# One block of a hybrid encoder in 3-pass fp32: first and last gate/up pair by products in turn, down's space in four pools, loads of the second half ahead of the last sums

## The chip, the cores and the metric

The kernel runs on one core of a Trainium2 chip. The metric is the time of one execution in device microseconds, the median of several runs. TensorE (PE) multiplies, VectorE (DVE), ScalarE (ACT) and GpSimd (POOL) do elementwise work, SyncE (SP) issues the DMAs of this part of the kernel. Each engine has a queue of its own and takes it in order.

## The reference

One layer with SEQ 2048, D 1024 and FF 2816 in float32; the kernel's third phase, which the change touches, ends it:

```python
x = x + merged @ w_out
h2 = rmsnorm(x, norm2_g)
x = x + (jax.nn.silu(h2 @ w_ffn_gate) * (h2 @ w_ffn_up)) @ w_ffn_down
return rmsnorm(x, norm_f_g)
```

Ahead of it stand an input projection, windowed attention and a bidirectional state-space scan, whose gated sum is `merged`.

## The kernel before

Products of fp32 matrices are made in three passes of fp32r (high by high, high by low, low by high). `hi_lo` (L828, L829) makes the two parts: ACT writes the rounded high part, DVE subtracts it for the low part. Names like H, w and zs are such pairs; `raw` is what a DMA brought. gate, up and down are computed with seven block products instead of eight, named BLK = ("11","S2","S1","12","S3","S4","22"); the operands S1 to S4 and the weights' block sums T (POOL, L847 to L850) are sums of quarters.

**Half by half.** The 2048 tokens are two halves of 1024. For each half `h_blocks` loads the seven H blocks from DRAM as 14 loads `hr` of 512 KB, each into one of three raw buffers that the weights' loads share, and splits them (14 roundings H on ACT, 14 on DVE). `gate_up` then goes through 22 units, that is 11 pairs of a gate unit and an up unit. A unit is seven products of 12 matmuls of 128x512. In `gu_unit` the products of "11" and "12" go to the PSUM tile ps_pj, "S2", "S3", "22" to ps_b, "S1" and "S4" to ps_a; between them c1 (L889, ACT), u2 (L892), c5 (L895), u3 (L900), u2 (L902) and, last, c1 (L907) take the partial sums out. Gate's results go through Silu on ACT (L944), up's are multiplied by them (L948). `z_blocks` makes from a pair the seven blocks of the next operand: three directly, four with sums on POOL (zsum, L926 to L931); each is split (zs) and stored to DRAM as z. `w_unit` loads, sums and splits the weights of a unit one unit ahead.

**Start of half 0.** The last quarter's x is normed by `norm_hs(3)`: four scalings of 128x1024 (L449 on ACT, L451 on DVE in the first phase), transposes on PE (L796), evictions hf (L797) and stores h. The first four H blocks are in before; S4 and 22 of them need h of this last quarter.

**Half 1's operand.** The sums S1 to S4 of half 1 are made by `h_sums_later` in four parts, after units 3, 6, 9 and 12 of half 0. After all of half 0 `h_blocks` asks for the H of half 1.

**Down.** `down` goes through 6 chunks of 8 units; a unit loads one z (three buffers, two units ahead) and makes seven products, in the first chunk of 3 matmuls each (4.8 us of TensorE a unit), later of 6. It keeps 16 tiles x and 8 tiles c1 over all chunks; the first chunk fills them (L1005, L1007, L1014).

**Space.** The pool gh holds the first four H blocks (8 x 8 KB a partition), gi the last three (6 x 8 KB), gt the tiles t (14 x 2 KB) and zs (3 x 4 KB). When they are closed, one pool "dn" takes their space for z, w3, x, c1, ct and gf. A tile of a new pool waits for every reader and writer of the space under that pool.

**Order.** The program is a list of instructions in the order of the code; a scheduler of the framework sets each engine's queue from it, by when operands come free. So the order on an engine isn't the code's word for word, but it is fixed when the kernel is built.

## Time and profile before

| | |
|---|---|
| median of 3 runs | 2749.73 us (2746.26 to 2751.05) |
| profiled execution | 2742.25 us, its span 2740.4 us |
| mean granted TensorE clock | 0.977 |
| PE busy | 2569.3 us, 94% |
| DVE, POOL, ACT busy | 1898.2, 1271.0, 1031.9 us |

The profile comes from one execution; its times within the span are used for differences, and a difference is set against the median. Gate/up of half 0 runs from about 1380 to 1860 us of the span, half 1 from there to 2281 us, down from there to the end. A wait is the idle time of an engine ahead of an instruction, with what ended it.

### The profile page before, as it was taken

The page shows a single profiled execution, that of the slowest core. Times are in us where ns is not written, and L with a number is a line of the kernel's source. Part 1 is how long each engine was busy: PE and PEld are TensorE (multiplying, and loading weights), DVE is VectorE, ACT ScalarE, POOL GpSimd, SP SyncE. Part 2 cuts the span into 40 slices and gives each one's busy share as a digit, 9 for nine tenths or more (in the row PEclk, how much of TensorE's full clock was granted, in tenths as well). Part 3 has the DMA queues.
Part 4 walks back from the last instruction along what each step waited for, and adds up shares of the span by engine and source line. Part 5 has one row for each costly group of instructions (what it writes and reads, how often), then busy time and mean ns, then how long its engine had stood idle before and what let it go on. Part 6 is the DMA issues. An engine that isn't in the chain of part 4 may idle for free.

```text
span 2740.4 us, 34681 instructions
## 1 busy us (share of the span) xinstructions
PE 2569.3 (94%) x12090; PEld 2115.4 (77%) x12090; DVE 1898.2 (69%) x2726; ACT 1031.9 (38%) x1877; POOL 1271.0 (46%) x1016
## 2 busy tenths in 40 slices
...
GB/s 161 98 143 183 183 128 74 94 78 105 77 176 180 184 170 146 165 203 238 188 211 169 177 180 172 155 180 199 154 152 150 162 155 200 254 270 253 217 190 257
DMA packets 451918, 467.95 MB, mean 171 GB/s; under 512 B 82848, under 2 KB 381856, under 8 KB 446624
## 3 DMA queue, kind: packets, MB, share of 16 engines
...
## 4 chain that ended last, share of the span: by engine, by line
PE 37%; DVE 5%; DMA 5%; POOL 4%; issue 3%; ACT 1%; SPq 0%; POOLq 0%; DVEq 0%; ACTq 0%
PE ps_b L876 15%; PE ps_a L876 10%; PE ps_pj L876 10%; DVE w L829 2%; DMA z<-z 1%; PE ps_pj L411 1%; DMA hr<-h 1%; PE ps_b L776 1%; PE ps_a L776 1%; POOL T L847 1%; DVE zs L829 1%; POOL T L848 1%; DMA raw<-in_w_ffn_up 1%; POOL T L849 1%; DVE H L829 1%
## 5 line engine op out<-in xcount | busy, mean ns | idle before, releaser
L411 PE MATMUL ps_pj<-h,w 128*128 128x512 f32 x1920 | 485.0, 401 | 0.0
L411 PEld LDWEIGHTS ps_pj<-h,w 128*128 128x128 f32 x1920 | 356.8, 189 | 79.1 <-issue 2.6
L876 PE MATMUL ps_b<-H,w 128*128 128x512 f32 x1584 | 386.4, 391 | 10.2 <-DVE u L892 5.2
L876 PEld LDWEIGHTS ps_b<-H,w 128*128 128x128 f32 x1584 | 297.7, 189 | 76.4 <-DVE u L900 7.9
L876 PE MATMUL ps_pj<-H,w 128*128 128x512 f32 x1056 | 265.0, 395 | 18.5 <-ACT c L889 17.7
L829 DVE TENSOR_TENSOR w<-T,w 128x512 fp32r<-128x512 f32 x220 | 205.1, 936 | 95.8 <-ACT w L828 93.5
L876 PE MATMUL ps_a<-H,w 128*128 128x512 f32 x1056 | 258.1, 390 | 1.0 <-ACT c L895 0.8
L876 PEld LDWEIGHTS ps_pj<-H,w 128*128 128x128 f32 x1056 | 200.4, 190 | 63.2 <-ACT c L889 20.1
L876 PEld LDWEIGHTS ps_a<-H,w 128*128 128x128 f32 x1056 | 198.2, 188 | 43.3 <-ACT c L895 2.2
L380 DVE TENSOR_TENSOR w<-raw,w 128x1024 fp32r<-128x1024 f32 x111 | 152.0, 1369 | 106.1 <-ACT w L377 77.2
L828 ACT ACTIVATE w<-T 128x512 fp32r<-128x512 f32 x220 | 136.0, 626 | 236.6 <-PE ps_b L876 74.7
L829 DVE TENSOR_TENSOR w<-raw,w 128x512 fp32r<-128x512 f32 x165 | 192.0, 1165 | 39.5 <-ACT w L828 39.5
L876 PE MATMUL ps_b<-w,z 128*128 128x512 f32 x792 | 202.8, 391 | 4.0 <-DVE xa L1009 3.1
L579 POOL TENSOR_SCALAR P<-P,st 128x384 f32<-128x384 f32 (+1 forms) x128 | 74.0, 597 | 270.6 <-DVE st L577 127.7
L876 PEld LDWEIGHTS ps_b<-w,z 128*128 128x128 f32 x792 | 148.6, 188 | 37.1 <-DVE xa L1009 4.5
L847 POOL TENSOR_TENSOR T<-raw 128x512 f32<-128x512 f32 x55 | 83.4, 1517 | 179.8 <-DVE w L829 117.4
L876 PE MATMUL ps_pj<-w,z 128*128 128x512 f32 x528 | 138.3, 393 | 19.8 <-DMA z<-z 19.2
L420 PE MATMUL ps_pj<-w,h 128*128 128x256 f32 x1152 | 147.7, 283 | 1.3 <-DVE h L463 0.8
L1009 DVE TENSOR_TENSOR xa<-xa,ps_b 128x512 f32<-128x512 f32 x128 | 87.1, 685 | 87.1 <-PE ps_b L876 85.4
L420 PEld LDWEIGHTS ps_pj<-w,h 128*128 128x128 f32 x1152 | 140.2, 188 | 3.5 <-issue 1.1
L571 DVE CUSTOM_DVE_ANT_0 P<-ps_a,cst,nsink 128x384 f32<-128x384 f32 (+1 forms) x128 | 74.1, 596 | 97.8 <-PE ps_a L569 97.4
L377 ACT ACTIVATE w<-raw 128x1024 fp32r<-128x1024 f32 x84 | 88.6, 1056 | 140.7 <-PE ps_pj L411 68.0
...
## 6 DMA issues: line engine op xcount, KB each, us to landing
...
```

The costliest lines, as they stand in the source:

```text
L377: self.s.activation(hi, src, AF.Copy)
L380: (lo_eng or self.v).tensor_tensor(lo, src, hi.bitcast(F32), SUB)
L411: self.pe.matmul(ps, W[a][:, k, cs], H[k][:, b, sl], start=(i == 0), stop=(i == n - 1))
L420: self.pe.matmul(ps, H[k][:, a, off:off + 128], W[k // 4][b][:, k % 4, :], start=(i == 0), stop=(i == n - 1))
L571: v.tensor_tensor_reduce(pt, sc, mk, -1.0, self.nsink[:, h:h + 1], ADD, ALU.min, nm[:, i:i + 1])
L579: p.tensor_scalar(P[i], P[i], den[:, i:i + 1], 1.0, MULT, MULT)
L776: self.pe.matmul(ps[t], M[k0 + k][:, a, 128 * t:128 * t + 128], W[b][:, k], start=(k0 + k + i == 0), stop=(k0 + k == 7 and i == 2))
L828: self.s.activation(hi, src, AF.Copy)
L829: self.v.tensor_tensor(lo, src, hi.bitcast(F32), SUB)
L847: eng.tensor_tensor(T[:, 0], b12, b11, SUB)
L876: self.pe.matmul(ps, a, b, start=(first and i == 0), stop=(i == n - 1), skip_group_check=True)
L1009: v.tensor_tensor(x[n], x[n], ps, ADD)
```

## The change

`gu_unit` becomes a generator that stops after each product. In the first and the last pair of each half (u = 0 and 20) gate's and up's products are taken in turn; for that up's weights and the next gate's are asked for ahead of the pair. The other pairs stay as they were. `gate_up` gets a function `after`, called after the last pair's products and ahead of its `z_blocks`: in half 0 it is `h_blocks` of half 1. `h_sums_later` comes after u = 2, 6, 10, 14, that is behind the pairs of units (2, 3), (6, 7), (10, 11) and (14, 15). In `norm_hs(3)` the four scalings of x and every second eviction hf go to DVE. Down's space is four pools: dz (three z) and dw (five w3) lie over gh, dm (x of the second half, ct, gf) over the end of gh and over gt, dx (x of the first half, c1) over gi. gf has three buffers.

```diff
--- before.py
+++ after.py
@@ -1,5 +1,6 @@
 import math
 from contextlib import ExitStack
+from itertools import zip_longest
 
 import numpy as np
 
@@ -58,6 +59,11 @@
     cst = np.concatenate([np.eye(128), mask, ka, km], 1)
     return (np.ascontiguousarray(rope.reshape(128, -1), dtype=np.float32),
             np.ascontiguousarray(cst, dtype=np.float32))
+
+
+def rest(gen):
+    for _ in gen:
+        pass
 
 
 class Kern:
@@ -435,7 +441,7 @@
         self.v.tensor_scalar(m, self.sumsq(x), 1.0 / D, 1e-6, MULT, ADD)
         return self.rsqrt(m)
 
-    def norm_x(self, src, tok, xs=None):
+    def norm_x(self, src, tok, xs=None, on_v=False):
 
         if xs is None:
             xs = []
@@ -445,7 +451,7 @@
                 xs.append(x)
         for x in xs:
             r = self.rstd(x)
-            if self.hi_on_act:
+            if self.hi_on_act and not on_v:
                 self.s.activation(x, x, AF.Copy, scale=r)
             else:
                 self.v.tensor_scalar(x, x, r, None, MULT)
@@ -786,7 +792,7 @@
     def norm_hs(self, q, X, g):
 
         hh, odd = divmod(q, 2)
-        self.norm_x(None, 0, X)
+        self.norm_x(None, 0, X, q == 3)
         for k in range(4):
             t = self.act.tile([128, 2, 512], F32, tag="a", name="hf")
             for i in range(2):
@@ -794,7 +800,10 @@
                 for j in range(4):
                     c = 128 * (k + 4 * i)
                     self.pe.transpose(pt[:, 128 * j:128 * j + 128], X[j][:, c:c + 128], self.ident)
-                self.s.activation(t[:, i], pt, AF.Identity, scale=g[:, k + 4 * i:k + 4 * i + 1])
+                if q == 3 and i:
+                    self.v.tensor_scalar(t[:, i], pt, g[:, k + 4 * i:k + 4 * i + 1], None, MULT)
+                else:
+                    self.s.activation(t[:, i], pt, AF.Identity, scale=g[:, k + 4 * i:k + 4 * i + 1])
                 if q != 1 or i:
                     self.store(self.hD[hh][f"{odd + 1}{i + 1}"][:, k], t[:, i])
             if q == 0:
@@ -887,20 +896,26 @@
         prod(A, "11", True, False)
         c1 = tl("c1")
         s.activation(c1, A, AF.Copy)
+        yield
         prod(B, "S2", True, False)
         u2 = tl("u2")
         v.tensor_tensor(u2, B, c1, ADD)
+        yield
         prod(C, "S1", True, False)
         c5 = tl("c5")
         s.activation(c5, C, AF.Copy)
+        yield
         prod(A, "12", False, True)
         fin("11", A)
+        yield
         prod(B, "S3", False, False)
         u3 = tl("u3")
         v.tensor_tensor(u3, B, c1, ADD)
+        yield
         prod(C, "S4", False, True)
         v.tensor_tensor(u2, C, u2, ADD)
         fin("12", u2)
+        yield
         prod(B, "22", False, True)
         p.tensor_tensor(u3, u3, c5, ADD)
         fin("22", u3)
@@ -932,26 +947,38 @@
         put("S3", Z["21"])
         put("S4", Z["12"])
 
-    def gate_up(self, tp, units, W, hh, H, nxt, bg):
+    def gate_up(self, tp, units, W, hh, H, nxt, bg, after=None):
+
 
         s, v, p = self.s, self.v, self.p
-        Z = {}
-        for u, (w, j) in enumerate(units):
-            Wn = self.w_unit(*units[u + 1]) if u + 1 < len(units) else nxt()
-            if u % 2 == 0:
-                def fin(n, z):
-                    g = tp.tile([128, 512], F32, tag="t", name="sg", bufs=14) if n == "11" else z
-                    s.activation(g, z, AF.Silu)
-                    Z[n] = g
+        n = len(units)
+        load = lambda u: self.w_unit(*units[u]) if u < n else nxt()
+        for u in range(0, n, 2):
+            Z = {}
+
+            def gate(n, z, Z=Z):
+                g = tp.tile([128, 512], F32, tag="t", name="sg", bufs=14) if n == "11" else z
+                s.activation(g, z, AF.Silu)
+                Z[n] = g
+
+            def up(n, z, Z=Z):
+                (p if n == "22" else v).tensor_tensor(Z[n], Z[n], z, MULT)
+
+            Wu = load(u + 1)
+            if u in (0, n - 2):
+                Wn = load(u + 2)
+                for _ in zip_longest(self.gu_unit(tp, W, H, gate), self.gu_unit(tp, Wu, H, up)):
+                    pass
             else:
-                def fin(n, z):
-                    (p if n == "22" else v).tensor_tensor(Z[n], Z[n], z, MULT)
-            self.gu_unit(tp, W, H, fin)
-            if u % 2:
-                self.z_blocks(tp, hh, j // 2, Z)
+                rest(self.gu_unit(tp, W, H, gate))
+                Wn = load(u + 2)
+                rest(self.gu_unit(tp, Wu, H, up))
+            if u == n - 2 and after:
+                H = after()
+            self.z_blocks(tp, hh, u // 2, Z)
             bg(u)
             W = Wn
-        return W
+        return W, H
 
     def wd_chunk(self, wd, j0, kc):
 
@@ -966,33 +993,33 @@
                 if self.nw % 16 < 11:
                     t = self.w_tile(self.nw % 16 if self.nw % 16 < 9 else 0, [128, 2, 512])
                 else:
-                    t = self.dp.tile([128, 2, 512], F32R, tag="w3", name="w", bufs=5)
+                    t = self.dw.tile([128, 2, 512], F32R, tag="w3", name="w", bufs=5)
                 self.nw += 1
                 self.hi_lo(t[:, 0], t[:, 1], src[n])
                 D7[n].append(t)
         return D7
 
-    def z_unit(self, dp, hh, c, tp, kc):
-
-        t = dp.tile([128, 7, 2, kc, 128], F32R, tag="z", name="z", bufs=3)
+    def z_unit(self, hh, c, tp, kc):
+
+        t = self.dz.tile([128, 7, 2, kc, 128], F32R, tag="z", name="z", bufs=3)
         self.load(t.bitcast(F32), self.zD[hh][c][tp])
         return {n: t[:, i] for i, n in enumerate(BLK)}
 
-    def down(self, dp, D7, wd, gfin, out):
+    def down(self, D7, wd, gfin, out):
         s, v, p = self.s, self.v, self.p
         X, C1 = {}, {}
         todo = [(c, hh, tp) for c in range(len(CHUNKS)) for hh in range(2) for tp in range(4)]
-        ahead = [self.z_unit(dp, hh, c, tp, CHUNKS[c][1]) for c, hh, tp in todo[:2]]
+        ahead = [self.z_unit(hh, c, tp, CHUNKS[c][1]) for c, hh, tp in todo[:2]]
         for u, (c, hh, tp) in enumerate(todo):
             first, last = c == 0, c == len(CHUNKS) - 1
             Z = ahead.pop(0)
             if u + 2 < len(todo):
                 c2, h2, t2 = todo[u + 2]
-                ahead.append(self.z_unit(dp, h2, c2, t2, CHUNKS[c2][1]))
+                ahead.append(self.z_unit(h2, c2, t2, CHUNKS[c2][1]))
             if first:
                 for t in (tp, tp + 4):
-                    X[hh, t] = dp.tile([128, D], F32, tag="x", name="xa", bufs=16)
-                C1[hh, tp] = dp.tile([128, 512], F32, tag="c1", name="c1", bufs=8)
+                    X[hh, t] = (self.dm if hh else self.dx).tile([128, D], F32, tag="x", name="xa", bufs=8)
+                C1[hh, tp] = self.dx.tile([128, 512], F32, tag="c1", name="c1", bufs=8)
             lo, hi = X[hh, tp], X[hh, tp + 4]
             x = {"11": lo[:, 0:512], "12": lo[:, 512:], "21": hi[:, 0:512], "22": hi[:, 512:]}
             c1 = C1[hh, tp]
@@ -1017,7 +1044,7 @@
                 for e, n in ((p, "12"), (p, "22"), (v, "21")):
                     e.tensor_tensor(x[n], x[n], c1, ADD)
             else:
-                t = dp.tile([128, 512], F32, tag="ct", name="ct", bufs=2)
+                t = self.dm.tile([128, 512], F32, tag="ct", name="ct", bufs=2)
                 s.activation(t, A, AF.Copy)
                 p.tensor_tensor(c1, c1, t, ADD)
             prod(B, "S2", True, False)
@@ -1041,7 +1068,7 @@
             if c == 3 and hh == 0 and tp == 0:
                 gf = []
                 for h in range(0, D, 512):
-                    t = dp.tile([128, 512], F32, tag="gf", name="gf", bufs=2)
+                    t = self.dm.tile([128, 512], F32, tag="gf", name="gf", bufs=3)
                     self.load(t, gfin[h:h + 512].partition_broadcast(128))
                     gf.append(t)
             if last:
@@ -1093,12 +1120,12 @@
             tp = self.pool("gt", 1, es)
             h2 = self.pool("gi", 1, es)
             H.update(self.h_blocks((h1, h2), 0, BLK[4:]))
-            W = self.gate_up(tp, units, W, 0, H, lambda: self.w_unit(*units[0]),
-                             lambda u: u in (3, 6, 9, 12) and self.h_sums_later(u // 3 - 1))
-            H = self.h_blocks((h1, h2), 1, BLK)
-            W = self.gate_up(tp, units, W, 1, H, lambda: self.wd_chunk(wd, *CHUNKS[0]), lambda u: None)
-        self.dp = dp = self.pool("dn", 1)
-        self.down(dp, W, wd, gfin, out)
+            W, H = self.gate_up(tp, units, W, 0, H, lambda: self.w_unit(*units[0]),
+                                lambda u: u in (2, 6, 10, 14) and self.h_sums_later(u // 4),
+                                lambda: self.h_blocks((h1, h2), 1, BLK))
+            W, H = self.gate_up(tp, units, W, 1, H, lambda: self.wd_chunk(wd, *CHUNKS[0]), lambda u: None)
+        self.dz, self.dw, self.dm, self.dx = (self.pool(n, 1) for n in ("dz", "dw", "dm", "dx"))
+        self.down(W, wd, gfin, out)
```

The lines move: L876 becomes L885, L828 and L829 become L837 and L838, L889 L898, L1014 L1041.

On PE at the start of half 0, before: w_12569 is gate's 12, w_12575 gate's S4, w_12572 gate's S3, w_12578 gate's 22; w_12755, w_12761, w_12758 and w_12764 are up's 11, S1, S2 and 12. First row of each product, in order:

```order
L876 MATMUL ps_pj_12776<-H_12613,w_12569 128x512 [waits Activation_49]
...
L876 MATMUL ps_a_12778<-H_12728,w_12575 128x512 [waits DMAHW3_49,DMAHW4_49,DMAHW2_49,DMAHW5_49,DMAHW1_49,DMAHW6_49,DMAHW0_49,DMAHW7_49,PE_49,Activation_49]
...
L876 MATMUL ps_b_12777<-H_12718,w_12572 128x512 [waits DVE_49]
...
L876 MATMUL ps_pj_12909<-H_12583,w_12755 128x512 [waits Activation_49]
...
L876 MATMUL ps_a_12911<-H_12603,w_12761 128x512 [waits Activation_49]
...
L876 MATMUL ps_b_12910<-H_12593,w_12758 128x512 [waits Activation_49]
...
L876 MATMUL ps_b_12777<-H_12738,w_12578 128x512 [waits DVE_49]
...
L876 MATMUL ps_pj_12909<-H_12613,w_12764 128x512 [waits Activation_49]
```

The same place after; w_12767, w_12770 and w_12773 are up's S3, S4 and 22:

```order
L885 MATMUL ps_pj_12806<-H_12613,w_12569 128x512 [waits Activation_49]
...
L885 MATMUL ps_pj_12823<-H_12583,w_12755 128x512 [waits Activation_49]
...
L885 MATMUL ps_a_12825<-H_12603,w_12761 128x512 [waits Activation_49]
...
L885 MATMUL ps_b_12824<-H_12593,w_12758 128x512 [waits Activation_49]
...
L885 MATMUL ps_pj_12823<-H_12613,w_12764 128x512 [waits Activation_49]
...
L885 MATMUL ps_b_12807<-H_12718,w_12572 128x512 [waits DMAHW4_49,DMAHW3_49,DMAHW5_49,DMAHW2_49,DMAHW6_49,DMAHW1_49,DMAHW7_49,DMAHW0_49,PE_49]
...
L885 MATMUL ps_b_12824<-H_12718,w_12767 128x512 [waits DVE_49,Activation_49]
...
L885 MATMUL ps_a_12808<-H_12728,w_12575 128x512 [waits Activation_49]
...
L885 MATMUL ps_a_12825<-H_12728,w_12770 128x512 [waits Activation_49]
...
L885 MATMUL ps_b_12807<-H_12738,w_12578 128x512 [waits DVE_49]
```

Up's 11 now stands directly behind gate's 12; gate's S3, S4 and 22 come behind up's 12, each ahead of up's.

On ACT at the boundary of the halves, before. H are the blocks of half 1, zs the last pair's blocks of half 0, c1_16287 the first copy of half 1, w_16251 the first of up's weights:

```order
L828 ACTIVATE zs_16138<-u2_15925 128x512 [waits DVE_49,Activation_49]
L828 ACTIVATE zs_16143<-u3_15967 128x512 [waits DMAHW2_49,Activation_49,Pool_49]
L828 ACTIVATE H_16224<-hr_16222 128x1024 [waits DMAHW6_49,PE_49]
L828 ACTIVATE H_16229<-hr_16227 128x1024 [waits DMAHW7_49,PE_49]
L828 ACTIVATE H_16234<-hr_16232 128x1024 [waits DMAHW2_49,PE_49]
L828 ACTIVATE zs_16150<-zsum_16131 128x512 [waits DMAHW4_49,Activation_49,Pool_49]
L889 ACTIVATE c1_16287<-ps_pj_16272 128x512 [waits PE_49]
L828 ACTIVATE H_16239<-hr_16237 128x1024 [waits DMAHW5_49]
L895 ACTIVATE c5_16315<-ps_a_16274 128x512 [waits PE_49]
L828 ACTIVATE zs_16156<-zsum_16132 128x512 [waits DMAHW0_49,DMAHW3_49,DVE_49,Pool_49]
L828 ACTIVATE w_16251<-raw_16242 128x512 [waits DMAHW6_49]
```

After; c1_16317 is the first copy, zs_16220, zs_16226, zs_16232 and zs_16237 are S1, S2, S3 and S4 of the last pair:

```order
L837 ACTIVATE H_16183<-hr_16181 128x1024 [waits DMAHW6_49,PE_49]
L837 ACTIVATE H_16188<-hr_16186 128x1024 [waits DMAHW1_49,PE_49]
L837 ACTIVATE zs_16220<-zsum_16201 128x512 [waits DMAHW7_49,Activation_49,Pool_49]
L898 ACTIVATE c1_16317<-ps_pj_16302 128x512 [waits PE_49]
L837 ACTIVATE zs_16226<-zsum_16202 128x512 [waits DMAHW2_49,DMAHW7_49,DVE_49,Pool_49]
L837 ACTIVATE H_16193<-hr_16191 128x1024 [waits DMAHW4_49]
L837 ACTIVATE zs_16232<-c1_15941 128x512 [waits DMAHW0_49,DMAHW3_49,DVE_49,Pool_49]
L837 ACTIVATE H_16198<-hr_16196 128x1024 [waits DMAHW5_49]
L837 ACTIVATE w_16251<-raw_16242 128x512 [waits DMAHW7_49]
L837 ACTIVATE zs_16237<-u2_15972 128x512 [waits DMAHW0_49,DMAHW6_49,DVE_49,Pool_49]
```

Two H roundings stand behind the first copy, where it was one; the first two blocks of the last pair are further ahead.

On SP at the passage from gate/up to down, before. zs_19569 to zs_19603 are blocks of the last pair, z_19614 to z_19618 down's first three loads:

```order
L72 DMA z15_9967<-zs_19569 128x4x128 [waits DMAHW1_49,Activation_49]
L72 DMA raw_19793<-in_w_ffn_down 128x1024 [waits DMAHW2_49,DVE_49,Pool_49]
L72 DMA z15_9967<-zs_19569 128x4x128 [waits DMAHW3_49,DVE_49]
...
L72 DMA z15_9967<-zs_19598 128x4x128 [waits DMAHW4_49,Activation_49]
L72 DMA z15_9967<-zs_19598 128x4x128 [waits DMAHW5_49,DVE_49]
L72 DMA z15_9967<-zs_19603 128x4x128 [waits DMAHW6_49,Activation_49]
L72 DMA z15_9967<-zs_19603 128x4x128 [waits DMAHW7_49,DVE_49]
L72 DMA z_19614<-z00_9956 128x1792 [waits DMAHW3_49,DMAHW4_49,DMAHW2_49,DMAHW5_49,DMAHW1_49,DMAHW6_49,DMAHW0_49,DMAHW7_49,PE_49,Pool_49]
L72 DMA z_19616<-z00_9956 128x1792
L72 DMA z_19618<-z00_9956 128x1792
```

After; z_19623 to z_19627 are the first three loads, z_19663 the fourth:

```order
L78 DMA raw_19772<-in_w_ffn_down 128x1024 [waits DMAHW7_49,DVE_49]
L78 DMA z_19623<-z00_9956 128x1792 [waits DMAHW0_49,PE_49]
L78 DMA z_19625<-z00_9956 128x1792 [waits DMAHW1_49]
L78 DMA z_19627<-z00_9956 128x1792 [waits DMAHW2_49]
L78 DMA z15_9967<-zs_19569 128x4x128 [waits DMAHW3_49,Activation_49]
L78 DMA z15_9967<-zs_19569 128x4x128 [waits DMAHW4_49,DVE_49]
...
L78 DMA z15_9967<-zs_19586 128x4x128 [waits Activation_49]
L78 DMA z15_9967<-zs_19586 128x4x128 [waits DMAHW6_49,DVE_49]
L78 DMA z15_9967<-zs_19592 128x4x128 [waits DMAHW7_49,Activation_49]
L78 DMA z_19663<-z00_9956 128x1792 [waits DMAHW0_49,PE_49]
...
L78 DMA z15_9967<-zs_19603 128x4x128 [waits DMAHW4_49,Activation_49]
L78 DMA z_19699<-z10_9962 128x1792 [waits DMAHW5_49,PE_49]
```

The first three loads stand ahead of all stores of the last pair and wait for PE alone; the fourth stands behind the stores of zs_19586 and the first of zs_19592.

## Rows read from the trace of the kernel before

**Rows 1.** Windows: us, busy us of each engine (count), granted clock, DMA share, GB/s
```profile
1380.00:1420.00 40.00, 29.38 (x128) 22.88 (x127) 17.76 (x22) 25.86 (x36) 1.65 (x3) 0.86 0.68 233
1420.00:1460.00 40.00, 36.66 (x147) 28.87 (x146) 30.93 (x33) 20.55 (x32) 23.46 (x15) 0.93 0.49 146
1500.00:1740.00 240.00, 232.33 (x1010) 188.51 (x1010) 189.49 (x198) 100.70 (x179) 166.41 (x105) 1.00 0.59 173
...
1820.00:1860.00 40.00, 36.76 (x160) 29.36 (x158) 33.69 (x34) 20.89 (x29) 13.07 (x8) 1.00 0.72 223
1860.00:1900.00 40.00, 31.61 (x130) 25.40 (x131) 32.42 (x32) 19.95 (x33) 28.53 (x18) 0.91 0.69 205
1900.00:2280.00 380.00, 380.00 (x1678) 314.89 (x1677) 294.97 (x323) 167.81 (x290) 241.66 (x152) 1.00 0.54 153
2260.00:2300.00 40.00, 22.06 (x96) 17.99 (x96) 25.99 (x32) 15.12 (x26) 20.78 (x14) 0.82 0.61 185
2300.00:2340.00 40.00, 39.22 (x165) 31.37 (x163) 18.10 (x27) 20.26 (x37) 2.82 (x3) 0.96 0.63 229
```

**Rows 2.** Page, groups of instructions: count | busy, mean ns | idle before, releaser
```profile
L876 PE MATMUL ps_pj<-H,w 128*128 128x512 f32 x1056 | 265.0, 395 | 18.5 <-ACT c L889 17.7
```

**Rows 3.** Waits of PE, 1385 to 1470: us in total, times, longest
```profile
PE ps_b L876 <- DVE u L892: 2.3, 1, 2.3
```

**Rows 4.** Timeline, start of half 0: start, us, engine, line, [idle before <-releaser]
```profile
1417.26 5.37 PE L876 MATMUL ps_pj<-H,w 128*128 128x512 f32 x12 [6.98 <-ACT c L889]
...
1422.30 3.42 SPq L72 DMA_DIRECT2D raw<-in_w_ffn_up  x2
...
1427.54 0.63 ACT L828 ACTIVATE w<-raw 128x512 fp32r<-128x512 f32 x1 [0.34 <-DMA raw<-in_w_ffn_up]
...
1428.22 0.73 PE L876 MATMUL ps_pj<-H,w 128*128 128x512 f32 x2
...
1434.51 1.78 DVE L829 TENSOR_TENSOR w<-raw,w 128x512 fp32r<-128x512 f32 x1
```

**Rows 5.** Line L451, scalings of x on DVE in the first phase: min/median/max ns
```profile
L451 DVE TENSOR_SCALAR x<-x,rs x16: 739/754/1581, 6.1 to 425.7; 128x1024 f32<-128x1024 f32 x16
```

**Rows 6.** Timeline of SP, then of all engines, at the boundary of the halves
```profile
1821.91 0.33 SPq L72 DMA_DIRECT2D hr<-h  x1
...
1859.97 0.90 SPq L72 DMA_DIRECT2D hr<-h  x1
1863.08 3.60 SPq L72 DMA_DIRECT2D raw<-in_w_ffn_up  x2
...
1858.13 0.68 DVE L907 TENSOR_TENSOR c<-ps_b,c 128x512 f32<-128x512 f32 x1
...
1865.64 0.58 ACT L889 ACTIVATE c<-ps_pj 128x512 f32<-128x512 f32 x1
...
1866.27 4.52 PE L876 MATMUL ps_pj<-H,w 128*128 128x512 f32 x12 [8.81 <-ACT c L889]
...
1871.31 1.73 POOL L847 TENSOR_TENSOR T<-raw 128x512 f32<-128x512 f32 x1
1871.82 1.77 DVE L829 TENSOR_TENSOR w<-raw,w 128x512 fp32r<-128x512 f32 x1
...
1878.63 0.68 DVE L829 TENSOR_TENSOR w<-raw,w 128x512 fp32r<-128x512 f32 x1
```

**Rows 7.** Timeline, passage from gate/up to down
```profile
2281.56 0.69 DVE L907 TENSOR_TENSOR c<-ps_b,c 128x512 f32<-128x512 f32 x1 [0.22 <-PE ps_b L876]
...
2284.20 1.58 POOL L926 TENSOR_TENSOR zsum<-c,u 128x512 f32<-128x512 f32 x1 [4.01 <-DVE c L948]
...
2290.49 0.63 ACT L828 ACTIVATE zs<-u 128x512 fp32r<-128x512 f32 x1 [1.04 <-POOL u L931]
...
2294.78 1.28 SPq L72 DMA_DIRECT2D z<-z  x3
...
2299.47 1.62 PE L876 MATMUL ps_pj<-w,z 128*128 128x512 f32 x3 [17.94 <-DMA z<-z]
```

## Prediction

> **What bounds the kernel now.** I read the windows first, then the page's groups of instructions, then the timeline of the three places that these point to. From 1900 to 2280 us, all of it gate and up of the second half, TensorE is busy 380.00 of 380 us with 1678 matmuls [rows 1]: 0.2265 us each, so a product of 12 matmuls is 2.72 us, one of the 14 products of a gate/up pair, and a pair takes 38.1 us. Nothing can be gained inside such a stretch, since the change removes no matmul. What can be gained is where TensorE waits, and the windows name the places: the start of the first half (1380 to 1460, 80 − 29.38 − 36.66 = 14.0 us not busy, some of it before the change's reach), the boundary between the halves (1820 to 1900, 80 − 36.76 − 31.61 = 11.6 us), and the passage from gate/up to down (2260 to 2300, 40 − 22.06 = 17.9 us), with 240 − 232.33 = 7.7 us spread over 1500 to 1740 [rows 1]. The page says the same by releaser: matmuls into ps_pj from H waited 18.5 us, nearly all for the copy c at L889 [rows 2], and the one long wait for z is 17.94 us [rows 7]. The granted clock adds to it. In the stretches with a long wait it is 0.82 to 0.93 against 1.00 in the steady one [rows 1]: after idling 6.98 us twelve matmuls took 5.37 us, after idling 8.81 us twelve took 4.52 [rows 4, 6], instead of 2.72. That is the 1.2 GHz level instead of 2.4, and it costs 1.8 to 2.7 us at each place.
>
> **Gate/up to down: the pools.** Before, the pool of down covers all of gh, gt and gi, so the first load of z waits until the last zs of the last pair is stored. The rows are a chain: DVE forms the last sum's operand at 2281.56, POOL starts zsum at 2284.20, ACT rounds the last block at 2290.49, SP issues the three loads of z at 2294.78, and TensorE starts 4.69 us later, at 2299.47, after idling 17.94 us [rows 7]. To this come about 3.3 us at the slow clock (clock 0.82 in 2260 to 2300 and 0.96 in 2300 to 2340 [rows 1]); together 21.2 us, the ceiling. Afterwards the three z buffers lie over gh alone, whose last reader is up's product 12, six products or 16.3 us before the end, and in SP's queue the three loads stand ahead of all zs stores of the last pair. Three loads of 896 KB at the 4.69 us of the row are there in time even one after another (14.1 us). So the first three units of down run straight on. What is late next: the fourth z stands in SP's queue behind three stores of sums that POOL forms only after the last product. From the last product to the last rounding is 2290.49 − 2281.5 = 9.0 us [rows 7]; ACT does the third of these stores after the third unit's first eviction, some 10 us after the end, and with 4.69 us for the load z is there at 14.7, while TensorE wants it after 62 matmuls, at 14.0. With a like delay for evictions that now stand among roundings on ACT and DVE I take 2.7 us of new waiting: gain 18.5. Bounds: 13 (every one of units 3 to 5 waits 2.7) and 21. The x of the second half, which still waits for the last stores, is wanted only at unit 4, 84 matmuls or 19 us on, against stores issued at about 13; I cost it at nothing, and if that cover is gone the 13 has room for it. The weights of down are rounded in the same order as before and the first seven stand before the last sums: nothing.
>
> Here a page speaks against the change. By the rows SP sends the z loads only when what they wait for is done (2294.78), and nothing of it while it waits [rows 7]. The Trainium skill, DMA: Bandwidth & Descriptors, section "Anatomy of one DMA", says that a semaphore wait happens on the issuing sequencer before dispatch, so a load that waits holds back everything behind it in the queue. By that rule the three early z loads hold the last pair's stores back until gh is free, and the fourth z is held by the stores; this is the third rival below.
>
> **Boundary between the halves.** Before, TensorE stops from 1857.46 to 1866.27 for the copy c of the first gate unit of half 1. ACT runs c at 1865.64 because in its queue it stands behind 13 of the 14 H roundings, and these go at the pace of the loads hr through three raw buffers: first at 1821.91, last at 1859.97, so 38.06 / 13 = 2.93 us each [rows 6]. Afterwards c stands behind 12 (one step, 2.9 us), and the requests stand ahead of z_blocks, so the chain has fewer stores and roundings in its way; I take 2.5 us for that (not shown; between 0 and the 8.8 of the whole wait). That puts c at about 1860.3, and the wait at 4.5 us instead of 8.8. Then the new thing: the second unit of the pair no longer comes after all of the first. TensorE's queue is in order, and up's 11 stands right behind gate's 12, with a wait for up's weights. The load of these still stands behind the last hr (1863.08), and their second half was rounded at 1871.82, late because DVE and POOL were at the last z sums; the last of the pair's products came to DVE only at 1858.13, since TensorE had put products of half 1 ahead [rows 6]. Now it comes first, so these sums are done some 10 us sooner. I put up's weights at 1865.6 to 1869.8, that is 2.5 to 6.8 us after gate's 12 has ended (1863). The loss then is 4.5 + 4.7 + 1.8 at the slow clock = 11 us; before it was 11.6 + 1.8 = 13.4 by the windows, with waits under 1 us and missing records some 14 to 15.5. The gain is 2.4 to 4.5; since the waits that end earlier are the surer part I take 4.5, with 1 and 11 as the ends (weights no sooner than 1870; both waits gone but for the slow clock).
>
> **Start of the first half.** Here the interleaving takes something away. Before, after gate's 12 (from 1417.26) TensorE had gate's S4 and S3 to run until up's weights came: load issued 1422.30, first rounding 1427.54, up's 11 from 1428.22 [rows 4]. After, up's 11 stands directly behind gate's 12, which ends at about 1422, and S3 and S4 of gate come later; TensorE idles some 5.5 us in their place. From there it is 8 products before (21.8 us), 10 after (27.2 us). Before: 1428.22 + 21.8 + 2.3 waiting for u [rows 3] + some 2.5 of smaller waits and slow clock = 1454.8. After: first product at 1427.6 (0.6 sooner, by the norm below), + 27.2, + 1.5 for the weights of the next blocks (the row at 1434.51 is the third block's second half, against a product wanted at 1433.9 [rows 4]) = 1456.3. Loss 1.5; bounds a gain of 1 (slow clock and wait for u both gone) and a loss of 4 (both stay, and the first product runs at half speed after the new idle time). Of the norm, four x scalings go from ACT to DVE, where one takes 0.754 us [rows 5], with four evictions. The loads h, hr and up's weights come behind them one after the other, so what the norm saves reaches up's 11; I take the 0.6 us used above, between 0 and 1.
>
> **Middle and the end pairs.** The sums for half 1 go from after units 3, 6, 9 and 12 to after 3, 7, 11 and 15: as many, each now right behind z_blocks, where POOL and DVE have work already. They stand for most of the 7.7 us [rows 1]; I take a loss of 1, from a gain of 3 to a loss of 4. The last pair of half 1 is interleaved too, but the steady stretch without a wait [rows 1] says that its weights are ready ahead: nothing, and if that fails it is inside the bounds of the boundary term.
>
> **Sum.** 18.5 + 4.5 − 1.5 − 1 = 20.5 us. The profiled execution took 2742.25 us, its span 2740.4 us, the median of the three runs 2749.73 us; I take the difference off the median: 2729 us (profiled about 2722). A difference of 0.2%, 5.5 us, is about what a measurement of this kernel can tell from none.
>
> **Rivals.**
> 1. The boundary closes and the start loses nothing, because hr and weights come sooner than I think: 18.5 + 11 + 1 = 30.5, 2719 us. For it: DVE and POOL are freed 10 us sooner; against it: hr still passes three buffers.
> 2. Up's weights eat the boundary's gain: 18.5 − 4 − 1 = 13.5, 2736 us. For it: the load issued only at 1863.08, behind the last hr.
> 3. z comes late all the same, behind stores in SP's queue, and evictions behind roundings on ACT hold TensorE: 3 of the 21.2 are won, with 4.5 − 1.5 − 1 it is 5 us, 2745 us. For it: one queue issues everything; against it: the three loads are ahead of the stores.
> 4. Slower: one mechanism, TensorE's in-order queue standing at up's products while gate's S3 and S4 are ready. Without that cover the start loses 5.5 us and 2.7 at half speed, 8.2; the boundary, with up's weights at 1873.6 (gate's 12 ended at 1869) and the next block's at 1879.3 as before [rows 6], 4.6 + 3 + 1.8 = 9.4; the middle 4. That is 21.6 against 18.5: 2753 us, and by the low end of the passage, 13, it is 2758. It makes the kernel slower by 5.5 us once the passage to down gives under 16.1.
>
> **How the numbers follow.** Forecast 0.54 (its own range 2724 to 2734), rival 1 0.16, rival 2 0.17, rival 3 0.09, rival 4 0.04. The ends of all four terms give 2714 (21 + 11 + 1 + 3 = 36) and 2744 (13 + 1 − 4 − 4 = 6); all at one end is unlikely, and the range 2714 to 2743 leaves out most of rival 3 and rival 4. Faster is below 2744.2, slower above 2755.2: forecast, rivals 1 and 2 and a little of rival 3 are faster, 0.88; the rest of rival 3 and part of rival 4 the same, 0.08; slower 0.04.
>
> **What would show it.** Right: no long wait for z in the page, the clock near 1.00 in the 40 us around the passage, at most 3 us of waits in down's first 20 us; the wait for c at the boundary about half, and a new wait of up's 11 for its weights there and at the start. Wrong: a wait for z over 5 us (rival 3), a wait for w of over 7 us at either start (rivals 2 and 4), none at all (rival 1), or waits in the last pair of half 1.

## The result and the profile after

| | before | after |
|---|---|---|
| median | 2748.14 us (4 runs, 2746.26 to 2751.05) | 2734.82 us (4 runs, 2731.56 to 2735.98) |
| ratio | | 0.9947, 95% interval 0.9931 to 0.9962 |
| profiled execution, its span | 2742.25, 2740.4 us | 2731.56, 2729.8 us |

The change makes the kernel some 13 to 15 us faster (10 to 19 by the ends of the interval). The prediction was 20.5 us. The time lies in its range, outside the forecast's own (2724 to 2734), next to rival 2's 2736, but not by rival 2's terms.

For where the time went I compare when the same count of gate/up or down matmuls starts. The start is the 1st to the 191st matmul of gate/up, the middle to the 1601st, the boundary to the 2101st, then a steady stretch to the 3401st, the passage from there to the 201st of down, and the rest of down. Differences to the kernel before, in us:

| kernel | start | middle | boundary | steady | passage | rest | sum | ratio (95% interval) |
|---|---|---|---|---|---|---|---|---|
| predicted | +1.5 | +1 | −4.5 | 0 | −18.5 | 0 | −20.5 | |
| after | 0.0 | −4.6 | +2.2 | 0 | −13.2 | +1.4 | −14.2 | 0.9947 (0.9931 to 0.9962) |
| pools_only | +0.1 | −0.7 | +0.4 | 0 | −14.4 | +0.8 | −13.8 | 0.9942 (0.9926 to 0.9957) |
| no_pools | +1.1 | −5.0 | +1.3 | 0 | −0.6 | +4.6 | +1.4 | 1.0011 (1.0000 to 1.0021) |
| first_seq | −3.3 | −3.5 | −3.9 | +0.4 | −11.9 | +2.1 | −20.1 | 0.9936 (0.9921 to 0.9951) |
| last_seq | +1.0 | −5.0 | +1.4 | 0 | −14.9 | +1.1 | −16.4 | 0.9948 (0.9930 to 0.9966) |
| none_seq | −3.6 | −2.6 | −0.3 | 0 | −13.7 | +1.0 | −19.3 | 0.9935 (0.9920 to 0.9950) |
| ahead_undone | +1.2 | −4.7 | +1.0 | 0 | −12.3 | +0.8 | −14.1 | 0.9936 (0.9920 to 0.9953) |
| sums_back | +2.2 | −1.7 | +1.7 | 0 | −12.7 | +1.9 | −8.6 | 0.9957 (0.9942 to 0.9972) |
| norm_act | +2.4 | −4.9 | +2.2 | 0 | −11.6 | +1.6 | −10.3 | 0.9955 (0.9940 to 0.9970) |
| first_seq_dve | −1.5 | −4.1 | −1.8 | 0 | −12.5 | +0.7 | −19.3 | 0.9927 (0.9913 to 0.9942) |
| one_turn | −1.8 | −1.9 | −4.6 | +0.9 | −15.0 | +0.5 | −21.9 | 0.9919 (0.9905 to 0.9933) |
| one_turn_late | −1.0 | −3.4 | −3.6 | +1.0 | −14.4 | +3.2 | −18.3 | 0.9935 (0.9923 to 0.9948) |
| one_turn_act | −2.8 | −3.3 | −3.6 | +0.9 | −15.4 | +4.4 | −19.8 | 0.9925 (0.9912 to 0.9939) |

Each row but the first rests on one profiled execution; the five kernels whose start is coded alike (after, no_pools, last_seq, ahead_undone, sums_back) spread over 2.2 us there, and first_seq and first_seq_dve, coded alike at the boundary, differ by 2.1 us there, so single entries under 2 us say little. Start and middle border on each other: the six kernels with the first pairs in sequence and the sums moved win more at the start and less in the middle, and over both stretches they are 3.7 to 6.7 us shorter than before, the four with the first pairs interleaved and the norm on DVE (after, no_pools, last_seq, ahead_undone) 3.5 to 4.6.

The windows of the kernel after, columns as in [rows 1]:

```profile
1420.00:1460.00 40.00, 34.52 (x136) 27.55 (x137) 28.96 (x33) 19.24 (x31) 23.11 (x15) 0.87 0.53 160
1500.00:1740.00 240.00, 237.06 (x1039) 194.22 (x1038) 194.95 (x198) 101.81 (x178) 167.64 (x106) 1.00 0.59 176
1820.00:1860.00 40.00, 36.16 (x147) 29.08 (x146) 30.88 (x34) 20.39 (x28) 11.65 (x8) 0.92 0.72 213
1860.00:1900.00 40.00, 33.84 (x134) 26.60 (x134) 29.74 (x34) 19.25 (x32) 29.55 (x19) 0.91 0.71 214
1900.00:2280.00 380.00, 380.00 (x1678) 314.78 (x1677) 292.11 (x320) 169.61 (x294) 238.45 (x151) 1.00 0.55 158
2260.00:2300.00 40.00, 35.70 (x156) 28.61 (x155) 35.36 (x40) 22.12 (x41) 25.63 (x17) 1.00 0.75 235
2300.00:2340.00 40.00, 38.93 (x160) 30.17 (x161) 17.14 (x26) 16.29 (x29) 2.51 (x2) 0.96 0.83 296
```

The steady stretch is as full as before (380.00). 2260 to 2300 went from 22.06 to 35.70 us busy and to the full clock; what is left there is 4.3 us, more of it beyond 2300. The middle went from 232.33 to 237.06. But 1420 to 1460 is emptier (34.52 against 36.66) and 1820 to 1860 has lost the full clock (0.92 against 1.00). The group of [rows 2] after, same columns:

```profile
L885 PE MATMUL ps_pj<-H,w 128*128 128x512 f32 x1056 | 266.2, 396 | 18.4 <-ACT w L837 8.8
```

The idle time before these matmuls is as long as it was (18.4 against 18.5 us), and half of it has a new releaser: w instead of c. Waits of PE after, at the start of half 0, at the boundary and at the passage (us in total, times, longest):

```profile
PE ps_pj L885 <- ACT c L898: 6.8, 1, 6.8
PE ps_pj L885 <- ACT w L837: 4.8, 1, 4.8
```
```profile
PE ps_pj L885 <- ACT w L837: 4.0, 1, 4.0
PE ps_b L885 <- DVE c L922: 3.2, 1, 3.2
PE ps_pj L885 <- ACT c L898: 1.4, 1, 1.4
```
```profile
PE ps_b L885 <- ACT xa L1032: 2.1, 1, 2.1
PE ps_a L885 <- DVE xa L1036: 1.9, 1, 1.9
PE ps_pj L885 <- DMA z<-z: 0.8, 2, 0.4
```

Both starts show the predicted new wait of up's 11 for its weights (4.8 and 4.0 us), the boundary also a wait of 3.2 us for an eviction (c L922) that was not predicted, and in place of 17.94 us for z [rows 7] there are two waits of about 2 us for evictions (xa). Of the signs that the prediction had named, the missing wait for z, the clock around the passage (1.00 and 0.96) and the new waits for w came; the waits in down's first 20 us are nearly 5 us, where at most 3 was said.

### The profile page after: what moved, and what is told of

Read it like the earlier page. It is cut to its first block, busy times and chain, and to the rows that moved or that the text cites. A ratio compares the mean times of both kernels' runs of the same rounds, so it can differ in the third digit from the quotient of the medians.

```text
span 2729.8 us, 34653 instructions
## 1 busy us (share of the span) xinstructions
PE 2572.3 (94%) x12090; PEld 2117.5 (78%) x12090; DVE 1905.8 (70%) x2734; ACT 1026.0 (38%) x1869; POOL 1259.4 (46%) x1016
## 4 chain that ended last, share of the span: by engine, by line
PE 71%; DVE 12%; POOL 6%; DMA 6%; issue 3%; ACT 1%; SPq 0%; DVEq 0%; POOLq 0%; ACTq 0%
PE ps_pj L417 17%; PE ps_b L885 16%; PE ps_pj L885 10%; PE ps_a L885 10%; PE ps_pj L426 4%; PE ps_a L782 3%; PE ps_b L782 3%; DVE w L838 2%; PE ps_c L601 1%; PE ps_b L594 1%; DVE W L357 1%; DMA z<-z 1%; POOL wn L207 1%; DVE w L386 1%; PE ps_a L574 1%
## 5 line engine op out<-in xcount | busy, mean ns | idle before, releaser
L885 PE MATMUL ps_b<-H,w 128*128 128x512 f32 x1584 | 385.2, 392 | 7.8 <-DVE u L913 3.5
L885 PEld LDWEIGHTS ps_b<-H,w 128*128 128x128 f32 x1584 | 298.3, 189 | 73.5 <-DVE u L913 5.6
L885 PE MATMUL ps_pj<-H,w 128*128 128x512 f32 x1056 | 266.2, 396 | 18.4 <-ACT w L837 8.8
L885 PE MATMUL ps_a<-H,w 128*128 128x512 f32 x1056 | 256.3, 390 | 0.0
L838 DVE TENSOR_TENSOR w<-T,w 128x512 fp32r<-128x512 f32 x220 | 204.6, 934 | 72.0 <-ACT w L837 70.1
L885 PEld LDWEIGHTS ps_pj<-H,w 128*128 128x128 f32 x1056 | 201.1, 191 | 63.8 <-ACT c L898 9.9
L885 PEld LDWEIGHTS ps_a<-H,w 128*128 128x128 f32 x1056 | 198.9, 188 | 41.4
L838 DVE TENSOR_TENSOR w<-raw,w 128x512 fp32r<-128x512 f32 x165 | 196.4, 1192 | 49.0 <-ACT w L837 48.8
L837 ACT ACTIVATE w<-T 128x512 fp32r<-128x512 f32 x220 | 136.2, 626 | 223.0 <-PE ps_b L885 71.6
L885 PE MATMUL ps_b<-w,z 128*128 128x512 f32 x792 | 203.9, 392 | 5.9 <-DVE xa L1036 3.3
L885 PEld LDWEIGHTS ps_b<-w,z 128*128 128x128 f32 x792 | 148.9, 189 | 40.0 <-DVE xa L1036 5.0
L837 ACT ACTIVATE w<-raw 128x512 fp32r<-128x512 f32 x165 | 103.0, 625 | 114.2 <-PE ps_pj L885 32.8
L885 PE MATMUL ps_a<-w,z 128*128 128x512 f32 x528 | 140.9, 392 | 3.4 <-DVE xa L1036 1.9
```

The costliest lines, as they stand in the source:

```text
L837: self.s.activation(hi, src, AF.Copy)
L838: self.v.tensor_tensor(lo, src, hi.bitcast(F32), SUB)
L885: self.pe.matmul(ps, a, b, start=(first and i == 0), stop=(i == n - 1), skip_group_check=True)
```

## The experiments

**The pools alone.** The kernel before with four pools for down (in `phase3`, `wd_chunk`, `z_unit` and `down`):

```diff
-        self.dp = dp = self.pool("dn", 1)
+        self.dz, self.dw, self.dm, self.dx = (self.pool(n, 1) for n in ("dz", "dw", "dm", "dx"))
```

> The kernel before with down's space in four pools and nothing else of the change. Theory (the parts act each at its own place and add up): the wait of 17.9 us for z goes and some 8 us of new waits come in down's first 20 us, as in the changed kernel; 12 to 14 us less at the passage, nothing elsewhere, about 2735 us. Rival (the interleaved last pair of half 1 is part of that gain or of those new waits): the passage differs from that of the changed kernel by 4 us or more, 2731 or 2740 us.

Measured 2731.63 us: the passage 14.4 us shorter, all else within 0.8. Waits of PE after the last product:

```profile
PE ps_pj L876 <- ACT c L1014: 2.0, 2, 1.4
PE ps_b L876 <- ACT xa L1005: 1.7, 1, 1.7
PE ps_pj L876 <- DMA z<-z: 1.4, 1, 1.4
```

The theory holds, and the pools alone give the whole of the change's gain. The new waits, 5 to 6 us, are there without any interleaving.

**The rest without the pools.** The changed kernel with one pool:

```diff
-        self.dz, self.dw, self.dm, self.dx = (self.pool(n, 1) for n in ("dz", "dw", "dm", "dx"))
+        self.dz = self.dw = self.dm = self.dx = self.pool("dn", 1)
```

> The changed kernel with one pool for all of down, as before; all else stays changed. Theory (the parts add up): the wait for z is back at 17 to 18 us and the rest of the change is worth 1 to 3 us against before, about 2746 us. Rival (the rest of the change gains at the start of the half and the boundary what the prediction said, 3 us net, and an unlucky profile hid it): 2743 us or less, with under 12 us lost at the boundary.

Measured 2749.60 us, as before or up to 0.2% slower. The wait for z is back (17.9 us). Both expectations hoped for more: 5.0 us won in the middle are lost again at the start, at the boundary and in down.

**The first pairs in sequence.**

```diff
-            if u in (0, n - 2):
+            if u == n - 2:
```

> The changed kernel, but the first pair of each half goes gate first, then up, as before; only the last pairs are interleaved. Theory (TensorE's queue stands at up's first product for up's weights while gate's S3, S4 and 22 are ready): the waits of 4.8 us at the start of half 0 and of 4.0 us at the boundary go, 2 to 3 us are gained at the start and 4 to 6 at the boundary, about 2728 us. Rival (the loads set the end of the pair, the wait only changes its place): the pair ends within 1.5 us of where it did, about 2734 us.

Measured 2729.77 us: 3.3 us less at the start and 6.1 less at the boundary than after. The waits for w are gone from both; at the boundary these are left:

```profile
PE ps_pj L885 <- ACT c L898: 3.7, 1, 3.7
PE ps_b L885 <- DVE c L922: 2.8, 1, 2.8
```

The theory holds: with gate's S3 and S4 between, TensorE has work while up's weights come.

**The last pairs in sequence.**

```diff
-            if u in (0, n - 2):
+            if u == 0:
```

> The changed kernel, but the last pair of each half goes gate first, then up, as before; only the first pairs are interleaved. Theory (in the last pair of half 0 the two units' evictions on DVE stand behind the H subtractions of half 1, which wait for their loads; interleaving puts two such evictions close together): the wait of 3.2 us for the last sums at the boundary and some 2.7 us at the slow clock go, 4 to 6 us gained there, the passage to down the same within 1.5 us, about 2730 us. Rival (the interleaved last pair does no harm; the H work ahead of the last evictions does, in any order of products): a wait of about 3 us for an eviction stays, 2734 us.

Measured 2733.30 us. The wait for the eviction went, but the boundary gained only 0.8 us, not 4 to 6, since the wait for c grew to 7.7 us and up's 11 still waited 2.0 for w. The passage is 1.7 us shorter. Neither side was right: the eviction's wait belongs to the interleaving, and removing it moves the time to c.

**No pair interleaved.**

```diff
-            if u in (0, n - 2):
+            if False:
```

> The changed kernel with no pair interleaved; pools, loads ahead, sums and norm stay changed. Theory (with the first pair undone the boundary is 3.5 us shorter than before because the loads are asked for ahead): the boundary is 3 to 4 us shorter than before, the start of half 0 3 us shorter, the passage as in the kernel with the pools alone, 13 to 14 us shorter; about 2728 us. Rival (the interleaved last pair makes that gain, since its sums and evictions end sooner): the boundary is within 1 us of before, about 2731 us.

Measured 2733.45 us. The boundary is as before (−0.3) and so is its wait:

```profile
PE ps_pj L885 <- ACT c L898: 9.1, 1, 9.1
```

So the rival holds. Asking ahead alone does not bring c forward (45.6 us after the 1729th gate/up matmul, before 45.1). The interleaved last pair of half 0 shortens the boundary, but only where the first pair of half 1 is in sequence (first_seq −3.9, first_seq_dve −1.8, one_turn −4.6; after +2.2). In these three c comes 0.3 to 1.4 us sooner than before, so c is only a part of it; where the rest comes from is not shown.

**H asked for behind the last sums again.**

```diff
-            if u == n - 2 and after:
-                H = after()
             self.z_blocks(tp, hh, u // 2, Z)
+            if u == n - 2 and after:
+                H = after()
```

> The changed kernel with half 1's H asked for behind the last sums of half 0, as before. Theory (asking ahead puts H subtractions on DVE ahead of the last evictions, which gives back what it saves): the wait of 3.2 us for the eviction goes, the wait for the copy c grows by 3 to 6 us, the first pair of half 1 ends within 2 us of where it did, about 2735 us. Rival (asking ahead brings the copy c forward by one step of the loads and more, as predicted): that pair ends 3 us or more later, 2738 us.

Measured 2733.00 us, the boundary within 1.2 us of the kernel after. From the 1729th gate/up matmul c comes 44.1 us on, in the kernel after 43.4, before 45.1: asking ahead is worth 0.7 us, not 3, and kernels coded alike there lie between 42.9 and 43.6. But the wait for the eviction stayed:

```profile
PE ps_pj L885 <- ACT c L898: 3.7, 1, 3.7
PE ps_b L885 <- DVE c L922: 2.9, 1, 2.9
```

So the theory's end was right and its mechanism wrong: the wait does not come from asking ahead.

**The sums of half 1 at their old places.**

```diff
                 rest(self.gu_unit(tp, W, H, gate))
+                bg(u)
...
-            bg(u)
+            bg(u + 1)
...
-                                lambda u: u in (2, 6, 10, 14) and self.h_sums_later(u // 4),
+                                lambda u: u in (3, 6, 9, 12) and self.h_sums_later(u // 3 - 1),
```

> The changed kernel with the sums for half 1 given out after units 3, 6, 9 and 12 again. Theory (between 1475 and 1804 us the changed kernel is 4.6 us shorter because a set of sums behind a gate unit holds up that pair's evictions and a set behind a pair does not): that stretch is 4 to 5 us longer again, all other stretches the same within 1 us, about 2739 us. Rival (the weights' loads asked for ahead of the pairs shortened it): under 1.5 us of it comes back, 2735 us.

Measured 2739.62 us. The middle is 2.9 us longer than after; 4 to 5 were expected. The places of the sums are the larger part of the middle's gain. A part of the other 1.7 us goes with the order of the first pair, with which the stretch begins: with the sums moved, the middle is 4.6 to 5.0 us shorter than before in the five kernels where that pair is interleaved, 1.9 to 4.1 in the six where it is in sequence.

**The norm on ACT.**

```diff
-        self.norm_x(None, 0, X, q == 3)
+        self.norm_x(None, 0, X)
...
-                if q == 3 and i:
+                if False:
```

> The changed kernel with the last quarter's x scaled on ACT and all evictions hf on ACT, as before. Theory (the norm on DVE gives 2.5 to 3.5 us at the start of half 0 and the interleaved first pair takes 3.5 to 4.5 away): the stretch 1361 to 1475 is 3 to 4 us longer than before, 2.5 to 3.5 longer than in the changed kernel, about 2737 us. Rival (the norm gives nothing, since up's weights set the end): that stretch is within 1 us of the changed kernel's, 2734 us.

Measured 2738.50 us, the start 2.4 us longer than after. But the four other kernels with the start of the kernel after are only 0.2 to 1.4 us shorter there than this one. So the norm on DVE is worth something between 0.2 and 2.4 us, hardly clear of this spread. The interleaved first pair costs more than that at the start: the six kernels with it in sequence are 1.0 to 3.6 us shorter at the start than before, the five with it interleaved 0.0 to 2.2 us longer, some 3.4 us between their means. Over start and middle together only some 1.5 us of it are left.

**The last sums on DVE.** On first_seq:

```diff
-        tt = self.p.tensor_tensor
+        tt = (self.v if hh and jp == 10 else self.p).tensor_tensor
```

> As first_seq (only the last pairs interleaved), and the four sums of the very last pair of half 1 run on DVE instead of POOL. Theory (at the passage POOL makes three block sums of down's weights ahead of the last pair's sums, their roundings on ACT come late and the evictions of down's first units stand behind these): the waits of 1.9 and 2.1 us and the wait for the fourth z shrink to under 1.5 us in all, the passage is 16 to 18 us shorter than before instead of 11.9, about 2725 us. Rival (DVE is the late engine there and the sums only lengthen its queue): the passage is no more than 13 us shorter than before, 2729 us or more.

Measured 2731.11 us. The passage is 12.5 us shorter than before, as the rival said. Two waits of 2 us became one:

```profile
PE ps_b L885 <- ACT xa L1032: 3.6, 1, 3.6
```

**Only one pair interleaved.**

```diff
-            if u in (0, n - 2):
+            if u == n - 2 and not hh:
```

> The changed kernel with only one pair interleaved, the last of half 0. Theory (interleaving pays only where the next half's work waits behind that pair, and costs 1 to 2 us at the passage to down): start of half 0 3 us shorter than before, the stretch 1475 to 1804 3.5 to 4.5, the boundary 2 to 3.5, the passage 13.5 to 15: 22 to 25 us against before in that part of the trace, about 2726 us. Rival (the passage is the same with and without interleaving, within 0.5 us of 12.5): 2729 us.

Measured 2727.16 us, 21.9 us in the trace. The passage is 15.0 and the boundary 4.6 us shorter; start and middle gave less than expected (1.8 and 1.9). It has the lowest median of all. By its runs (2725.17 to 2729.08) it lies below the kernel before and below the kernel after (2731.56 to 2735.98), but its interval overlaps with that of the pools alone (0.9905 to 0.9933 against 0.9926 to 0.9957): what it gains over them, 8 us in the trace, the whole times do not show for sure. The passage is 13.7 to 15.4 us shorter in the six kernels where the last pair of half 1 is in sequence, 11.6 to 13.2 in the six where it is interleaved.

**Weights of the second chunk held back.** On one_turn; POOL writes a column of each raw buffer from x ahead of the load:

```diff
+                if gate is not None:
+                    self.p.tensor_tensor(r[i][:, 0, 0:1], gate[:, 0:1], gate[:, 0:1], ADD)
                 self.load(r[i], wd[256 * j + 128 * i:256 * j + 128 * i + 128, :].rearrange("p (c d) -> p c d", d=512))
```

> As one_turn, and the four loads of the weights of down's second chunk are held back until the second unit of down has written its x (POOL writes one column of each raw buffer from that x ahead of the load; the load overwrites it). Theory (what is left at the passage comes from preparing those weights there, 14 low parts on DVE and 8 sums on POOL, among the last pair's sums and down's first evictions): the waits in the first 25 us of down shrink from about 5 us to under 2, the passage is 17 to 20 us shorter than before, about 2722 us, if the weights still come in time for unit 8, 38 us after the last product. Rival (the last pair's own chain of sums, roundings and stores sets it, or the weights come late for unit 8): the passage is no more than 15 us shorter or the gain comes back as a wait for w near 2320, 2726 us or more.

Measured 2730.10 us, slower than one_turn. The windows 2280 to 2320 of one_turn, then of this kernel, columns as above:

```profile
2280.00:2300.00 20.00, 15.44 (x63) 10.97 (x62) 17.03 (x23) 10.07 (x19) 13.16 (x9) 1.00 1.01 292
2300.00:2320.00 20.00, 19.21 (x85) 15.60 (x84) 6.94 (x11) 10.29 (x18) 0.00 (x0) 1.00 0.83 277
```
```profile
2280.00:2300.00 20.00, 17.85 (x77) 13.89 (x77) 11.22 (x17) 11.14 (x20) 6.03 (x7) 1.00 1.03 328
2300.00:2320.00 20.00, 17.70 (x72) 14.16 (x71) 14.75 (x21) 11.71 (x22) 12.10 (x9) 0.91 0.88 303
```

The first 20 us are 2.4 us fuller, with DVE down from 17.03 to 11.22 us and POOL from 13.16 to 6.03: those weights do stand in the way there. The next 20 us lose 1.5 us of it again at a lower clock (0.91), and the 201st matmul of down comes 0.6 us later against before than in one_turn (−14.4, −15.0); the rest of down loses 2.7 more. On the timeline, a weight's low part on DVE beside POOL's sums, then an eviction, then PE:

```profile
2304.44 1.78 DVE L838 TENSOR_TENSOR w<-raw,w 128x512 fp32r<-128x512 f32 x1
...
2307.81 0.67 DVE L1038 TENSOR_TENSOR xa<-xa,ps_b 128x512 f32<-128x512 f32 x1
...
2308.54 0.78 PEld L885 LDWEIGHTS ps_b<-w,z 128*128 128x128 f32 x3 [2.73 <-DVE xa L1038]
```

The wait moved to a later place; it was not removed.

**One eviction from DVE to ACT.** On one_turn:

```diff
-            add("11", A, v)
+            add("11", A, s)
```

> As one_turn, and in down's first chunk the eviction of product 12 into x (DVE, 0.69 us a unit) goes to ACT. Theory (DVE, busy 17 to 19.5 of 20 us behind the last product, is the engine on which down's first evictions queue; ACT is busy 10 to 12 of 20): the passage is 16 to 17.5 us shorter than before instead of 15, about 2725 us. Rival (the evictions wait because ACT's roundings of the last pair's sums wait for POOL; one more eviction behind these makes it worse): the passage is 12 to 15 us shorter, 2727 to 2730 us, with waits for ACT.

Measured 2729.05 us; the passage 15.4 us shorter, little more than 15.0, with a wait for ACT as the rival said:

```profile
PE ps_b L885 <- ACT xa L1032: 2.0, 1, 2.0
```

So it isn't DVE alone; on ACT the evictions stand among roundings, which wait up to 1.80 us for POOL's sums (2291.12).

## Why the prediction was right and where it was wrong

**Passage, −18.5 predicted, −13.2 measured, +1.4 later.** The mechanism was right (no_pools has the 17.9 us again, pools_only has the gain), the term for new waits was mis-sized: 2.7 us, measured about 8 of the ceiling of 21.2. The ceiling was itself too high by some 1.5 us: I put 3.3 us on the slow clock, but before, only the first nine matmuls of down run slowly (1.62, 1.48 and 1.24 us for three each, against 0.84), 1.8 us in all. Without a ceiling: at 0.2265 us a matmul the 496 steps of this stretch take 112.3 us; before took 22.4 us more, the kernel after 9.2. I had read the order of SP, ACT and DVE there, not POOL's. The timeline after, PE's waits among the rows of the other engines:

```profile
2266.41 2.47 SPq L78 DMA_DIRECT2D z<-z  x3
...
2285.91 1.28 POOL L856 TENSOR_TENSOR T<-raw 128x512 f32<-128x512 f32 x1 [4.89 <-DVE w L838]
...
2287.14 1.75 POOL L858 TENSOR_TENSOR T<-raw 128x512 f32<-128x512 f32 x1
...
2288.85 1.74 POOL L857 TENSOR_TENSOR T<-raw,T 128x512 f32<-128x512 f32 x1
...
2290.55 1.29 POOL L941 TENSOR_TENSOR zsum<-c,u 128x512 f32<-128x512 f32 x1
...
2292.54 1.53 DVE L838 TENSOR_TENSOR zs<-zsum,zs 128x512 fp32r<-128x512 f32 x1
...
2294.73 0.96 PE L885 MATMUL ps_a<-w,z 128*128 128x512 f32 x3 [1.89 <-DVE xa L1036]
...
2295.24 0.63 ACT L837 ACTIVATE zs<-zsum 128x512 fp32r<-128x512 f32 x1 [2.25 <-POOL zsum L942]
...
2296.35 0.46 SPq L78 DMA_DIRECT2D z<-z  x1
...
2298.18 0.63 ACT L837 ACTIVATE zs<-u 128x512 fp32r<-128x512 f32 x1 [1.06 <-POOL u L946]
...
2298.72 1.06 ACT L1032 ACTIVATE xa<-ps_b 128x512 f32<-128x512 f32 x2
...
2299.84 0.99 PE L885 MATMUL ps_b<-w,z 128*128 128x512 f32 x3 [2.09 <-ACT xa L1032]
...
2300.64 1.47 PE L885 MATMUL ps_a<-w,z 128*128 128x512 f32 x3
```

POOL makes three block sums T of the second chunk's weights ahead of the first zsum and a fourth behind it, so the last rounding comes 15.5 us after the end of the last product (2298.18 − 2282.70), where before it was 9.0 [rows 7]. ACT waits 2.25 us and again 1.06 us for such sums (2295.24, 2298.18), and the evictions xa of 2298.72, with which PE's wait of 2.09 us ends, stand behind the second of these roundings. On DVE the eviction that ends the wait of 1.89 us stands behind a low part of zs (2292.54). SP behaved as predicted: the first three z loads went out at 2266.41 and the fourth, behind the stores, at 2296.35, 13.7 us after the last product instead of 10, and still there were only 0.8 us of waits for z. The Trainium skill, DMA: Bandwidth & Descriptors, section "Anatomy of one DMA", says that a semaphore wait happens on the issuing sequencer before dispatch, and the trace agrees: the fourth load goes out 0.48 us after the end of the rounding (2295.24) for which the store ahead of it waits. But this queue was not the one that set the time. "The last pair of half 1 is interleaved too: nothing" was also wrong: it costs the passage about 2 us (13.7 to 15.4 us gained without it, 11.6 to 13.2 with it).

**Boundary, −4.5 predicted, +2.2 measured.** The step that failed is c at 1860.3, 5.3 us sooner: "one step, 2.9 us" and "the requests stand ahead of z_blocks, so the chain has fewer stores and roundings in its way; I take 2.5 us for that". With it failed "Now it comes first, so these sums are done some 10 us sooner": the products do come first, their evictions do not. After, the loads hr (first and last start), then the timeline:

```profile
L78 SPq DMA_DIRECT2D hr<-h x6: 319/332/463, 1823.0 to 1861.1; - x6
```
```profile
1844.84 2.59 PEld L885 LDWEIGHTS ps_b<-H,w 128*128 128x128 f32 x12 [1.04 <-DVE u L913]
...
1851.49 1.06 ACT L837 ACTIVATE H<-hr 128x1024 fp32r<-128x1024 f32 x1 [1.99 <-DMA hr<-h]
1852.58 1.22 DVE L838 TENSOR_TENSOR H<-hr,H 128x1024 fp32r<-128x1024 f32 x1 [0.95 <-ACT H L837]
1853.72 0.68 DVE L922 TENSOR_TENSOR c<-ps_b,c 128x512 f32<-128x512 f32 x1
...
1854.46 5.49 PE L885 MATMUL ps_b<-H,w 128*128 128x512 f32 x12 [3.21 <-DVE c L922]
...
1857.51 0.68 DVE L922 TENSOR_TENSOR c<-ps_b,c 128x512 f32<-128x512 f32 x1
...
1859.25 0.69 DVE L965 TENSOR_TENSOR c<-c,c 128x512 f32<-128x512 f32 x1
...
1862.99 0.58 ACT L898 ACTIVATE c<-ps_pj 128x512 f32<-128x512 f32 x1
...
1869.98 0.63 ACT L837 ACTIVATE w<-raw 128x512 fp32r<-128x512 f32 x1 [2.48 <-DMA raw<-in_w_ffn_up]
...
1870.66 1.22 PE L885 MATMUL ps_pj<-H,w 128*128 128x512 f32 x2 [4.03 <-ACT w L837]
...
1872.65 4.64 PE L885 MATMUL ps_pj<-H,w 128*128 128x512 f32 x10 [0.77 <-DVE w L838]
```

I count from the start of the 1729th gate/up matmul (1820.57 before, 1819.57 after). The loads hr run from 3.5 to 41.5 us, where before they ran from 1.3 to 39.4 [rows 6]: the chain is 2 us later, not 2.5 sooner. The requests stand earlier in the code, but the loads still wait for raw buffers: the second goes out at 1827.24, when DVE has ended the low part of the last pair's weights in that buffer (1825.43 to 1827.21). In none_seq, where H is asked for ahead as well, the first load goes out at 1.3 us as before. So of the two terms only the one step is left, and c runs 1.7 us sooner, not 5.3. That is 3.6 of the 6.7 us by which the boundary was missed. From c to the 2101st matmul the kernel after takes 3.8 us longer than before; by the prediction's terms it would have been 0.8.

The last pair's final product starts at 1844.84; its eviction, the second c L922, runs at 1857.51. DVE takes its queue in order and stands at H subtractions, each behind a rounding that waits for its load (1851.49, 1852.58). So what the last sums are made of is ready (1859.25) 39.7 us after the 1729th matmul, where it was 42.4: 2.7 us sooner, not 10. Up's weights, behind the same chain, are first rounded at 1869.98, 50.4 us after it, where before it was 48.1 (1868.64); the prediction had put them at 45 to 49. And with two pairs of products at DVE at once, TensorE lacks a PSUM tile for 3.2 us. That wait stayed with H asked for late (ahead_undone) and went with the last pair in sequence (last_seq, none_seq). The new wait for w had its cause right (first_seq takes it away) and its size (4.7 predicted, 4.0 measured, with 0.8 more for a low part). The slow clock, priced at one product, falls on two: the twelve matmuls at 1854.46 take 5.49 us and the next twelve behind the wait for w 1.22 and 4.64, where before only those at 1866.27 were slow (4.52) [rows 6].

**Start, +1.5 predicted, 0.0 measured** (+1.0 to +2.2 in the four other kernels with the same start). Near in sum, with the interleaving's part too small: it costs about 3.4 at the start, not 2.1. What the norm gives, predicted 0.6, is not shown more closely than between 0.2 and 2.4.

**Middle, +1 predicted, −4.6 measured.** The sign was wrong. I argued that sums right behind z_blocks meet a busy POOL and DVE; in fact the stretch is fuller, and sums_back takes 2.9 us of it back.

**Sum.** Passage and boundary were put 5.3 and 6.7 us too good and the rest of down 1.4, the middle 5.6 and the start 1.5 too bad: 14.2 instead of 20.5. The time lies inside the range by luck as well: these errors cancel in part. Of the rivals, number 1 was refuted. Number 2's mechanism held at the boundary (with up's products behind gate's, first_seq gains 6.1 us there), but its price of 13.5 was nearly met only because the passage and the middle missed by like amounts in opposite directions. Number 3's late z was refuted (0.8 us of waits), its evictions behind roundings are what was seen, at some 4 us and not 18. The mechanism of number 4 is real (3.3 us at the start and 6.1 at the boundary by first_seq), far from its price of 21.6.
